# Last key tile's value products of two heads in one 256-column matmul, in free columns of the scores' PSUM tile

## The chip, the cores and the metric

The kernel runs on one core of one Trainium2 chip. The metric is the device time of one execution in microseconds (us); the time of a kernel is the median of several runs. The engines are named as in the profile: PE (TensorE, matmuls; PEld its weight loads), DVE (VectorE), ACT (ScalarE), POOL (GpSimd), and SP, whose queue starts most of the transfers. Each engine executes its instructions in the order in which the program has them, and waits at semaphores for the others.

## What is computed

One decoder layer on 512 tokens of width 2048, in float32: an RMS norm, native sparse attention (16 heads of 128 columns, 4 key and value groups), a SwiGLU feed-forward, and a final norm. The part that matters here is attention, cut down from the reference:

```python
s_c = einsum('btghd,bcgd->bghtc', q, kcc) + bias_c      # compressed keys
p_c = masked_softmax(s_c, mask_c)
o_c = einsum('bghtc,bcgd->btghd', p_c, vcc)
...
s = einsum('bqghd,bgqkd->bghqk', qc, kg) + bias         # selected keys
p = masked_softmax(s, dist >= 0)
o_s = einsum('bghqk,bgqkd->bqghd', p, vg)
...
s_w = einsum('bjqghd,bjkgd->bjghqk', qw, kwb) + bias_w  # sliding window
p_w = masked_softmax(s_w, mask_w)
o_w = einsum('bjghqk,bjkgd->bjqghd', p_w, vwb)
o = gates[0] * o_c + gates[1] * o_s + gates[2] * o_w
return o @ w_out
```

With 512 tokens both the selected and the windowed branch see every earlier key, so both are plain causal attention with a bias, each with keys and values of its own.

## The kernel before, in words

Float32 values are split into a high and a low part, and each product is made as three matmuls (`three`, lines 354 to 357): high by high, high by low, low by high. On PE's rows these are lines L355, L356 and L357 in turn; the first two use the same weights.

Heads 0 to 15 are worked through by a loop of 12 steps per head (`STEPS`), written out by hand near the end of the attention stage (lines 1039 to 1069). In one head's steps, work of three kinds is laid out:

- For the next head, `scores` (line 934) makes the score products of one query tile of 128 tokens into the PSUM tile `s`, 1536 columns wide, which exists once; DVE adds the bias and finds the maximum (L954), ACT takes the exponential (L956). Query tiles 3, 2, 1, 0 are done at steps 2, 5, 8, 11. Tile 3 fills columns 224 to 1279 of `s`, tile 2 columns 224 to 1023, tile 1 columns 736 to 1279. `finish` (line 959) scales by the gates (L967), transposes (L968) and sends the probabilities out to memory (`d_p`) on SP; `fetch` (line 972) brings them back, turned, into `ptr`.
- For the head itself, `turn` (line 981) splits the turned probabilities of one branch and one key tile into `pth` (ACT, L991) and `ptl` (DVE, L995), at steps 0 to 8; `values` (line 998) multiplies them by the values two steps later, steps 2 to 9 and 11, all into one PSUM tile `o`. The key tiles come in the order 3, 2, 1, 0, each for both branches: key tile 3 is seen by the last 128 queries alone (128 columns), key tile 2 by 256, then 384 and 512. There are three buffers of `pth` and two of `ptl`: the `ptl` of a step is written into the buffer that the value products of the same step have read. `head_out` (line 1011) copies `o` into the tile `stage` at step 11 (ACT, L1015) and SP sends it to `d_o` (heads 0 to 11).
- In between, `pump` (line 885) lays in a stretch of the dense projections (PE rows `proj`), by a count of nanoseconds per head that depends on the head and the step alone; with them go ACT's and DVE's splits of the weights (`whi`, `wlo`, L104 and L105) and, for queries and keys, a scaling into `yt` (L410) and its split.

`partial` (line 845), after the projections, makes a part of the output projection of heads 0 to 11 and stages it in a tile of 1024 columns of the same name `stage`.

Of the kernel before, what the change touches and what calls it, by code (L numbers as in the profile page):

```python
# [10 lines left out]
F32 = mybir.dt.float32  # L11
F32R = mybir.dt.float32r
I32 = mybir.dt.int32
AF = mybir.ActivationFunctionType
OP = mybir.AluOpType
# [4 lines left out]
S, D, H, DH, G, HPG = 512, 2048, 16, 128, 4, 4  # L20
NT, KC = S // 128, D // 128
# [204 lines left out]
def nsa_block(ctx: ExitStack, tc: tile.TileContext, x, rel_bias, mix_g, ffn_g, fin_g, w_in, w_out,  # L226
              pos_k, w1k, w2k, pos_v, w1v, w2v, f_in, f_out, onehot, out):
    nc = tc.nc
    mm, act, dve, pool = nc.tensor.matmul, nc.scalar.activation, nc.vector, nc.gpsimd
# [22 lines left out]
    d_o = [dram.tile([4, 128, S], F32, name=f"d_o{i}") for i in range(3)]  # L252
    d_h = dram.tile([S, 256 * N_SPILL], F32, name="d_h")
# [39 lines left out]
    def tok(t):  # L293
        return slice(128 * t, 128 * (t + 1))
# [59 lines left out]
    def three(o, ah, al, bh, bl, start, stop):  # L354
        mm(o, ah, bh, start=start, stop=False, skip_group_check=True)  # L355
        mm(o, ah, bl, start=False, stop=False, skip_group_check=True)  # L356
        mm(o, al, bh, start=False, stop=stop, skip_group_check=True)  # L357

    def ws(ps, gi, g, c0=0, c1=S, start=None, end=None, of=None):

        for u in range(2):
# [3 lines left out]
            for k in range(4):  # L365
# [5 lines left out]
                    later(lambda u=u: end(u))  # L371
                yield 650

    def later(f):
        (W.later or (lambda f: f()))(f)

# [13 lines left out]
    keep = mixer.enter_context(tc.tile_pool(name="keep", bufs=1))  # L390
# [9 lines left out]
    KK, VV, Q = {}, {}, {}  # L400
# [5 lines left out]
    kv_tiles(keep, 0)  # L406

    def normed(p, scale=1.0):
        t = keep.tile([128, S], F32, name="yt", bufs=2)
        dve.scalar_tensor_tensor(t, p, scale, ybc, op0=OP.mult, op1=OP.mult)  # L410
        return t

# [37 lines left out]
    with ExitStack() as st1:  # L450
# [4 lines left out]
        def proj_tiles(n=2):  # L455
            return [(psx if next(turns) % 4 > 1 else ps1).tile([128, 512], F32, name="proj") for _ in range(n)]
# [5 lines left out]
        with ExitStack() as st0:  # L462
# [35 lines left out]
            def bank(shape):  # L498
                return ps1.tile(shape, F32, name=next(names))
# [49 lines left out]
            p = bank([128, 512])  # L549
# [34 lines left out]
            ps = proj_tiles()  # L584
            for q in range(4):
# [23 lines left out]
                if q == 3:  # L609
                    p = bank([128, S])  # L610
# [71 lines left out]
        ps = proj_tiles()  # L682
# [3 lines left out]
        ps = proj_tiles()  # L686
# [7 lines left out]
        ps, hk = proj_tiles(), ps1.tile([128, 256], F32, name="mlp")  # L694
# [8 lines left out]
        ps = proj_tiles()  # L703
# [5 lines left out]
        ps, hv = proj_tiles(4), ps1.tile([128, 256], F32, name="mlp")  # L709
        ge = cp.tile([128, NT, 3, H], F32, name="ge")  # L710
        for i in range(8):
# [10 lines left out]
            if i == 1:  # L722
                p = ps1.tile([128, 128], F32, name="tr")
# [16 lines left out]
        ps = proj_tiles()  # L740
# [10 lines left out]
        p = ps1.tile([96, G, 128], F32, name="tr")  # L751
# [8 lines left out]
    with ExitStack() as st2:  # L760
        ap_ = st2.enter_context(tc.tile_pool(name="ap", bufs=2))
# [21 lines left out]

        W.later = lambda f: held.append((done["ns"], f))

        def stage_tile():
            return ap_.tile([128, 1024], F32, name="stage", bufs=1)

        units = iter(range(1000))

        def proj2():
            pool_ = (psx, ps2)[next(units) % 2]
            return [pool_.tile([128, 512], F32, name="proj") for _ in range(2)]
# [42 lines left out]
        def reload_o(i):  # L836

            nc.sync.dma_start(hn_l[:, i].bitcast(F32), d_o[i // 4][i % 4])

        def split_o(k):  # L840
            h, l = (x[:, 2 * k:2 * k + 2] for x in (hn_h, hn_l))
            act(h, l.bitcast(F32), AF.Copy)  # L842
            dve.tensor_tensor(l, l.bitcast(F32), h.bitcast(F32), op=OP.subtract)  # L843

        def partial(cb):
            st = stage_tile().rearrange("p (t c) -> p t c", t=NT)
            c = slice(256 * cb, 256 * (cb + 1))
            ps = [p.rearrange("p (t c) -> p t c", t=2) for p in proj2()]
            for i in range(3):
                w = W.take()  # L850
                for t in range(NT):
                    if not cb and i == 0 and t < 3:
                        reload_o(9 + t)
                    if not cb and i < 2 and t % 2 == 0:
                        later(lambda i=i, t=t: split_o(2 + 2 * i + t // 2))
                    if i == 2 and t == 2:
                        later(lambda n=W.nt + 3: W.until(n))
                    for k in range(4):
                        h = 4 * i + k
                        three(ps[t // 2][:, t % 2], hn_h[:, h, tok(t)], hn_l[:, h, tok(t)], w[0][:, k], w[1][:, k],  # L860
                              h == 0 and t % 2 == 0, h == 11)
                        if k % 2:
                            yield 650
                    if i == 2 and t % 2:
                        b = t // 2
                        act(st[:, 2 * b:2 * b + 2], ps[b], AF.Copy)
            pool.dma_start(d_h[:, c].rearrange("(t p) c -> p t c", p=128), st)
            later(pair_done)
            yield None

# [40 lines left out]

        TB, HS = {}, {}
        sc = ps2.tile([128, 3, 512], F32, name="s", bufs=1).rearrange("p a c -> p (a c)")

        def load_bias(h):
            if h < H:
# [59 lines left out]
        def arrived(rows, c0, t0, step):  # L976
            v = PT[:rows, :, c0:c0 + 32]
            p, i, c = v.ap
            return bass.AP(tensor=v.tensor, offset=v.offset, ap=[p, [step, NT - t0], i, c])

        def turn(h, b, kt):
            n = S - 128 * kt
            th = ap_.tile([128, 512], F32R, name="pth", bufs=3)
            tl = ap_.tile([128, 512], F32R, name="ptl") if b >= 0 else th
            rows = 128 if b >= 0 else 96
            if b < 0:
                src = arrived(rows, 64, 0, PT_STEP + 64)
            else:
                src = arrived(rows, PT_STEP * kt + 32 * (kt + 1) * b + 32 * kt, kt, PT_STEP + 32 * b)
            th4, tl4 = (x[:rows, :n].rearrange("p (t i s) -> p t i s", i=4, s=32) for x in (th, tl))  # L990
            act(th4, src, AF.Copy)  # L991
            if b < 0:
                dve.tensor_tensor(th4[32:64], src[32:64], th4[32:64].bitcast(F32), op=OP.subtract)
            else:
                dve.tensor_tensor(tl4, src, th4.bitcast(F32), op=OP.subtract)  # L995
            HS[h]["t", b, kt] = th[:rows, :n], tl[:rows, :n]

        def values(h, b, kt):
            s, g = HS[h], h // HPG
            first = "o" not in s  # L1000
            if first:
                s["o"] = ps2.tile([128, 512], F32, name="o", bufs=1)
            th, tl = s.pop(("t", b, kt))
            o = s["o"][:, 128 * kt:]
            if b < 0:
                mm(o, vcc[:, g], th, start=first, stop=True, skip_group_check=True)
            else:
                vh, vl = (v[:, kt, 128 * b:128 * (b + 1)] for v in VV[g % 2])
                three(o, vh, vl, th, tl, first, False)

        def head_out(h):
            o = HS[h]["o"]
            if h < 12:
                f = stage_tile()[:, :S]
                act(f, o, AF.Copy)  # L1015
                nc.sync.dma_start(d_o[h // 4][h % 4], f)
            else:
                split_from(o, hn_h[:, h], hn_l[:, h])
            del HS[h]
# [19 lines left out]
        for h in range(H):  # L1039
            seq = [(b, kt) for kt in (3, 2, 1, 0) for b in (0, 1)] + [(-1, 0)]  # L1040
            for i in range(STEPS):
                if i == 4:
                    load_bias(h + 2)
                if i == 2 and h:
                    fetch(0)
                if i < 9 and (h or i > 1):
                    turn(h, *seq[i])
                if i == 8 and h + 1 < H:
                    fetch(3)
                    fetch(2)  # L1050
                if i == 11 and h + 1 < H:
                    fetch(1)
                if i == 0 and h:
                    finish(h, 0)
                if h + 1 < H:
                    if i == 2:
                        drain_to(needed(h + 1))
                    if i % 3 == 2 and h + i > 2:
                        scores(h + 1, 3 - i // 3)
                    elif i % 3 == 0 and i:  # L1060
                        finish(h + 1, 4 - i // 3)
                if 2 <= i < 10 or i == 11:
                    if i == 2 and h % HPG == 0:
                        drain_to(h)
                    values(h, *seq[min(i - 2, 8)])
                    if i == 11:
                        head_out(h)
                if h or i > 1:
                    pump(h, i)
# [137 lines left out]

    def sub(o, a, b):
        dve.tensor_tensor(o, a, b, op=OP.subtract)  # L1209

    def plus(o, a, b):
        dve.tensor_tensor(o, a, b, op=OP.add)  # L1212

    S4 = {}

# [432 lines left out]
    n, pending = 0, None  # L1648
    for s, (b, js, _) in enumerate(PASSES):
# [6 lines left out]
        for i, j in enumerate(units):  # L1656
# [4 lines left out]
            if pending is not None:  # L1661
                o = accb["now"] = late2.tile([128, NT, 512], F32, name="accb")
# [47 lines left out]
        o = accb["now"]  # L1710
# [110 lines left out]
```

## Time and profile before

| what | value |
|---|---|
| median of 3 runs | 2091.55 us (2089.91 to 2093.0) |
| the profiled execution, its time | 2092.27 us |
| its span in the profile | 2090.5 us |
| PE busy | 2072.8 us (99%), 15220 matmuls |
| weight loads busy | 1952.6 us (93%) |
| DVE busy | 1629.2 us (78%) |
| ACT busy | 948.3 us (45%) |

The times in a timeline are counted from the start of the span. The attention loop lies between about 200 and 690 us. A matmul's row shows how long it is in flight; since matmuls overlap, what one costs in a stream is read from the distance of the starts.

### The profile page before, as it was taken

What the parts mean: (1) busy time and instruction counts of PE and PEld (TensorE: products, weight loads), DVE (VectorE), ACT (ScalarE), POOL (GpSimd) and SP (SyncE); (2) the same over time, 40 slices, a digit from 0 to 9 for tenths busy, and PEclk for the clock granted to TensorE, in tenths of its full rate; (3) what the DMA queues carried; (4) which work ended last, traced back from release to release, by engine and by line L of the source; (5) the groups of instructions that cost most, each with busy time, mean ns of one, the idle gap of its engine ahead of it and who ended that gap; (6) DMA issues with size and microseconds to landing.
All of it is one profiled execution on the core that took longest, in us unless ns stands there. A gap on an engine that the chain in (4) does not pass through costs nothing.

```text
span 2090.5 us, 39010 instructions
## 1 busy us (share of the span) xinstructions
PE 2072.8 (99%) x15220; PEld 1952.6 (93%) x15220; DVE 1629.2 (78%) x2640; ACT 948.3 (45%) x1522; POOL 275.2 (13%) x400
## 2 busy tenths in 40 slices
PE   9999999999999999999999999999999999999998
PEld 7898898898989889899999999999999999999997
DVE  5565777777786367898898888888988688697767
ACT  6344454555554234444434344334343455464445
POOL 2000011111111001022122132221211100000000
PEclk9999999999999999999999999999999999999999
DMA  7555766667677668578878688788755686685677
GB/s 239 180 148 155 195 192 195 192 198 202 201 221 212 234 204 227 164 211 230 212 214 223 190 231 218 201 229 215 199 156 151 222 265 183 198 293 156 186 208 275
DMA packets 324309, 429.77 MB, mean 206 GB/s; under 512 B 40379, under 2 KB 252027, under 8 KB 323356
## 3 DMA queue, kind: packets, MB, share of 16 engines
q1 hardware_dynamic: 263852, 295.32, 45.2%
q0 software_dynamic: 59376, 130.11, 25.8%
q8 instruction: 119, 1.95, 0.4%
q10 hardware_dynamic: 896, 1.84, 0.2%
q14 instruction: 66, 0.54, 0.1%
HBM read 364.17 MB, written 131.18 MB: 237 GB/s over the span
## 4 chain that ended last, share of the span: by engine, by line
PE 68%; DVE 1%; ACT 0%; DMA 0%; issue 0%; DVEq 0%; ACTq 0%
PE f L356 19%; PE f L355 19%; PE f L357 19%; PE proj L355 2%; PE proj L356 2%; PE proj L357 2%; PE pp L357 1%; PE pp L355 1%; PE pp L356 1%; PE po L356 1%; PE po L355 1%; PE po L357 1%; DMA tlo<-in_ffn_w_out 0%; PE pp L333 0%; DVE slot L1212 0%; PE o L356 0%
## 5 line engine op out<-in xcount | busy, mean ns | idle before, releaser
L105 DVE TENSOR_TENSOR wlo<-raw,whi 128x1024 fp32r<-128x1024 f32 (+2 forms) x223 | 247.5, 1112 | 123.0 <-ACT whi L104 122.6
L104 ACT ACTIVATE whi<-raw 128x1024 fp32r<-128x1024 f32 (+2 forms) x223 | 215.7, 971 | 224.8 <-PE f L357 70.0
L357 PE MATMUL f<-hn_h,wlo 128*128 128x256 f32 x984 | 271.6, 276 | 0.0
L355 PE MATMUL f<-hn_h,whi 128*128 128x256 f32 x984 | 271.6, 276 | 0.0
L356 PE MATMUL f<-hn_l,whi 128*128 128x256 f32 x984 | 271.6, 276 | 0.0
L1313 ACT ACTIVATE whi<-raw 128x1024 fp32r<-128x1024 f32 x123 | 126.1, 1058 | 301.6 <-DVE raw L1209 298.2
L1209 DVE TENSOR_TENSOR tlo<-tt,thi 128x1536 fp32r<-128x1536 f32 (+1 forms) x83 | 145.4, 1752 | 80.3 <-ACT thi L1318 78.7
L355 PE MATMUL proj<-hn_h,whi 128*128 128x512 f32 x504 | 200.0, 397 | 0.0
L357 PE MATMUL proj<-hn_h,wlo 128*128 128x512 f32 x504 | 196.9, 391 | 0.0
L356 PE MATMUL proj<-hn_l,whi 128*128 128x512 f32 x504 | 196.6, 390 | 0.0
L356 PEld LDWEIGHTS f<-hn_l,whi 128*128 128x128 f32 x984 | 184.7, 188 | 0.0
L355 PEld LDWEIGHTS f<-hn_h,whi 128*128 128x128 f32 x984 | 184.7, 188 | 0.0
L357 PEld LDWEIGHTS f<-hn_h,wlo 128*128 128x128 f32 x984 | 184.7, 188 | 0.0
L1318 ACT ACTIVATE thi<-tt 128x1536 fp32r<-128x1536 f32 x82 | 121.9, 1486 | 74.3 <-PE f L356 74.3
L356 PE MATMUL f<-tlo,slot 128*128 128x256 f32 (+1 forms) x546 | 151.7, 278 | 0.0
L355 PE MATMUL f<-thi,slot 128*128 128x256 f32 (+1 forms) x546 | 151.6, 278 | 0.0
L357 PE MATMUL f<-thi,slot 128*128 128x256 f32 (+1 forms) x546 | 151.6, 278 | 0.0
L357 PE MATMUL proj<-whi,hn_l 128*128 128x256 f32 (+2 forms) x496 | 146.4, 295 | 2.6 <-DVE hn_l L843 2.6
L355 PE MATMUL proj<-whi,hn_h 128*128 128x256 f32 (+2 forms) x496 | 146.6, 296 | 0.8 <-ACT hn_h L842 0.8
L1209 DVE TENSOR_TENSOR wlo<-raw,whi 128x1024 fp32r<-128x1024 f32 x123 | 147.1, 1223 | 0.0
L356 PE MATMUL proj<-wlo,hn_h 128*128 128x256 f32 (+2 forms) x496 | 145.8, 294 | 0.0
L356 PE MATMUL f<-wlo,slot 128*128 128x256 f32 (+1 forms) x432 | 121.5, 281 | 0.0
(411 smaller groups left out, 6454.5 us busy)
## 6 DMA issues: line engine op xcount, KB each, us to landing
raw<-in_ffn_w_in SPq DMA_DIRECT2D x135, 512.0 KB, 5.4
d_w<-in_ffn_w_out POOLq DMA_DIRECT2D x80, 512.0 KB, 8.8
rawx<-in_ffn_w_in SPq DMA_DIRECT2D x41, 512.0 KB, 5.3
raw<-in_ffn_w_out SPq DMA_DIRECT2D x73, 256.0 KB, 3.7
tlo<-d_w SPq DMA_DIRECT2D x73, 256.0 KB, 4.5
d_a<-d_a POOLq DMA_DIRECT2D x120, 128.0 KB, 5.8
slot<-d_a SPq DMA_DIRECT2D x18, 768.0 KB, 7.1
raw<-in_nsa_w_in POOLq DMA_DIRECT2D x24, 512.0 KB, 4.8
```

The lines of the kernel that those rows point to most:

```text
L104: self.nc.scalar.activation(hi[:, :n], src, AF.Copy)
L105: self.nc.vector.tensor_tensor(lo[:, :n], src, hi[:, :n].bitcast(F32), op=OP.subtract)
L355: mm(o, ah, bh, start=start, stop=False, skip_group_check=True)
L356: mm(o, ah, bl, start=False, stop=False, skip_group_check=True)
L357: mm(o, al, bh, start=False, stop=stop, skip_group_check=True)
L1209: dve.tensor_tensor(o, a, b, op=OP.subtract)
L1313: act(h, r, AF.Copy)
L1318: act(h, ttf, AF.Copy)
```

## The change

For heads 0 to 11 the value products of key tile 3 leave `values`. The high and low parts of an even head and the odd head behind it are put side by side into two new tiles of 512 columns (`x3` and, from the place that `stage` gives up, `stage2`). At step 4 of the odd head `last_values` makes the products of both heads, 256 columns wide, into the columns 1280 to 1535 of `s`, as six matmuls. `join_last` adds one head's 128 columns to its copy in `stage` on DVE and then sends the copy out: for the even head right behind `last_values`, for the odd head at its step 11, in `head_out`. `stage` becomes two tiles of 512 columns, and `partial` uses both, each with a transfer of its own on POOL. `yt` has one buffer instead of two.

```diff
     def normed(p, scale=1.0):
-        t = keep.tile([128, S], F32, name="yt", bufs=2)
+        t = keep.tile([128, S], F32, name="yt", bufs=1)
...
-        def stage_tile():
-            return ap_.tile([128, 1024], F32, name="stage", bufs=1)
+        def stage_tile(name="stage", dtype=F32):
+            return ap_.tile([128, 512], dtype, name=name, bufs=1)
...
         def partial(cb):
-            st = stage_tile().rearrange("p (t c) -> p t c", t=NT)
+            st = [stage_tile(x).rearrange("p (t c) -> p t c", t=2) for x in ("stage", "stage2")]
...
-                        act(st[:, 2 * b:2 * b + 2], ps[b], AF.Copy)
-            pool.dma_start(d_h[:, c].rearrange("(t p) c -> p t c", p=128), st)
+                        act(st[b], ps[b], AF.Copy)
+            for b in range(2):
+                pool.dma_start(d_h[256 * b:256 * (b + 1), c].rearrange("(t p) c -> p t c", p=128), st[b])
...
+        ox = sc[:, 1280:]
+        last = [x.rearrange("p (b n c) -> p b n c", b=2, n=2)
+                for x in (ap_.tile([128, 512], F32R, name="x3", bufs=1), stage_tile("stage2", F32R))]
...
+        def paired(h, kt):
+
+            return h < 12 and kt == 3
+
         def turn(h, b, kt):
             n = S - 128 * kt
-            th = ap_.tile([128, 512], F32R, name="pth", bufs=3)
-            tl = ap_.tile([128, 512], F32R, name="ptl") if b >= 0 else th
+            if paired(h, kt):
+                th, tl = (x[:, b, h % 2] for x in last)
+            else:
+                th = ap_.tile([128, 512], F32R, name="pth", bufs=3)
+                tl = ap_.tile([128, 512], F32R, name="ptl") if b >= 0 else th
...
+        def join_last(h):
+
+            f = outs.pop(h)
+            plus(f[:, 384:], f[:, 384:], ox[:, 128 * (h % 2):128 * (h % 2 + 1)])
+            nc.sync.dma_start(d_o[h // 4][h % 4], f)
+
+        def last_values(h):
+
+            for b in range(2):
+                three(ox, *(v[:, 3, 128 * b:128 * (b + 1)] for v in VV[h // HPG % 2]),
+                      *(x[:, b].rearrange("p n c -> p (n c)") for x in last), b == 0, b == 1)
+            join_last(h - 1)
+
         def head_out(h):
             o = HS[h]["o"]
             if h < 12:
-                f = stage_tile()[:, :S]
+                f = outs[h] = stage_tile()
                 act(f, o, AF.Copy)
-                nc.sync.dma_start(d_o[h // 4][h % 4], f)
+                if h % 2:
+                    join_last(h)
...
-                    values(h, *seq[min(i - 2, 8)])
+                    if i == 4 and h % 2 and h < 12:
+                        last_values(h)
+                    if i > 3 or h >= 12:
+                        values(h, *seq[min(i - 2, 8)])
```

The change has its own line numbers: `turn`'s split on DVE is L1009 there (L995 before), the transpose L975 (L968), the bias and maximum L961 (L954), and the sum `plus` is L375. In brackets stand the engines whose counters an instruction waits for.

DVE, head 1, from step 3 to step 5, before. The transposed tile `p_1874` is that of `finish` at step 3, the two 128x384 rows are `turn` at steps 4 and 5, and the last row begins the reductions of query tile 2's scores:

```order
L968 STREAM_TRANSPOSE p_1874<-p_1874 128x1152 [waits DVE_49]
L105 TENSOR_TENSOR wlo<-raw,whi 128x1024 [waits DMASW2_49,Activation_49]
L995 TENSOR_TENSOR ptl<-ptr,pth 128x384 [waits DMAHW1_49,PE_49,Activation_49]
L995 TENSOR_TENSOR ptl<-ptr,pth 128x384 [waits PE_49,Activation_49]
L954 ISA cx_1877,mx<-s,biasc 128x31
```

And in the change:

```order
L975 STREAM_TRANSPOSE p_1874<-p_1874 128x1152 [waits DVE_49]
L105 TENSOR_TENSOR wlo<-raw,whi 128x1024 [waits DMASW2_49,Activation_49]
L1009 TENSOR_TENSOR ptl<-ptr,pth 128x384 [waits DMAHW1_49,PE_49,Activation_49]
L375 TENSOR_TENSOR stage<-stage,s 128x128
L1009 TENSOR_TENSOR ptl<-ptr,pth 128x384 [waits PE_49,Activation_49]
L961 ISA cx_1877,mx<-s,biasc 128x31
```

The sum of head 0's last columns has come between the two `ptl`. The second `ptl` waits, as before, for PE's value products of step 5.

PE, head 1, step 4, before (the value products of key tile 2, first branch, then the dense work):

```order
L355 MATMUL o<-pth,v0h 128x256 [waits Activation_49]
L356 MATMUL o<-ptl,v0h 128x256 [waits DVE_49]
L357 MATMUL o<-pth,v0l 128x256
L355 MATMUL proj<-hn_h,whi 128x512
L356 MATMUL proj<-hn_l,whi 128x512
```

And in the change, where `x_1893` is the tile `x3` and `stage_1894` the tile `stage2`:

```order
L355 MATMUL s<-x_1893,v0h 128x256 [waits DVE_49,Activation_49]
L356 MATMUL s<-stage_1894,v0h 128x256
L357 MATMUL s<-x_1893,v0l 128x256
L355 MATMUL s<-x_1893,v0h 128x256 [waits Activation_49]
L356 MATMUL s<-stage_1894,v0h 128x256
L357 MATMUL s<-x_1893,v0l 128x256
L355 MATMUL o<-pth,v0h 128x256 [waits PE_49,Activation_49]
L356 MATMUL o<-ptl,v0h 128x256
L357 MATMUL o<-pth,v0l 128x256
L355 MATMUL proj<-hn_h,whi 128x512
```

Six matmuls into `s` have come ahead of step 4's value products; the first waits for the last reduction of query tile 3's scores. The triples `o<-pth,v0h 128x128` of steps 2 and 3 are gone.

PE, head 1, step 5, in the change (before, the rows read alike):

```order
L357 MATMUL proj<-hn_h,wlo 128x512
L355 MATMUL s<-k0h,qh 128x288 [waits DVE_49]
L356 MATMUL s<-k0l,qh 128x288
L357 MATMUL s<-k0h,ql 128x288
L355 MATMUL s<-k0h,qh 128x512
```

The score products of query tile 2 wait for DVE in both programs. Before, the count that they wait for is reached with the last reduction of query tile 3's scores; in the change it is reached with the sum at L375. The same holds in heads 3, 5, 7, 9 and 11. At step 2 of the heads behind an odd head, the score products of query tile 3 wait in the same way for the odd head's own sum.

## Rows read from the trace of the kernel before

**Rows 1.** The page, part 1: busy us (share of the span) x instructions.
```profile
PE 2072.8 (99%) x15220; PEld 1952.6 (93%) x15220; DVE 1629.2 (78%) x2640; ACT 948.3 (45%) x1522; POOL 275.2 (13%) x400
```
**Rows 2.** Window 230 to 575: us, then PE, PEld, DVE, ACT, POOL, PEclk, DMA, GB/s.
```profile
230.00:575.00 345.00, 343.34 (x1957) 302.22 (x1956) 269.88 (x709) 178.73 (x479) 49.26 (x66) 1.00 0.69 195
```
**Rows 3.** Timeline of PE, head 1, steps 3 and 4: start, us, engine, line, instruction.
```profile
251.78 0.22 PE L355 MATMUL o<-pth,v0h 128*128 128x128 f32 x1
251.84 0.27 PE L356 MATMUL o<-ptl,v0h 128*128 128x128 f32 x1
...
252.35 0.40 PE L356 MATMUL proj<-hn_l,whi 128*128 128x512 f32 x1
252.59 0.39 PE L357 MATMUL proj<-hn_h,wlo 128*128 128x512 f32 x1
...
253.50 0.28 PE L355 MATMUL o<-pth,v0h 128*128 128x256 f32 x1
...
254.09 0.39 PE L356 MATMUL proj<-hn_l,whi 128*128 128x512 f32 x1
```
**Rows 4.** Timeline, head 1: DVE's `ptl` of steps 3 to 5, PE's products of step 5.
```profile
253.66 0.43 DVE L995 TENSOR_TENSOR ptl<-ptr,pth 128x256 fp32r<-128x256 f32 x1 [1.29 <-ACT pth L991]
...
255.94 0.29 PE L355 MATMUL s<-k0h,qh 128*128 128x288 f32 x1
...
257.90 1.02 DVE L995 TENSOR_TENSOR ptl<-ptr,pth 128x384 fp32r<-128x384 f32 x2
```
**Rows 5.** Groups by shape, DVE, 205 to 575: busy us, mean ns, idle before.
```profile
L995 DVE TENSOR_TENSOR ptl<-ptr,pth 128x384 fp32r<-128x384 f32 x24 | 12.3, 549 | 0.5 <-PE o L356 0.5
...
L995 DVE TENSOR_TENSOR ptl<-ptr,pth 128x128 fp32r<-128x128 f32 x25 | 7.1, 287 | 20.2 <-ACT pth L991 20.2
```
**Rows 6.** Timeline, head 11, the two places of rows 4.
```profile
552.66 0.29 PE L355 MATMUL s<-k1h,qh 128*128 128x288 f32 x1
...
555.41 1.02 DVE L995 TENSOR_TENSOR ptl<-ptr,pth 128x384 fp32r<-128x384 f32 x2
```
**Rows 7.** Timeline of DVE, step 0 of heads 9 and 10.
```profile
485.38 0.29 DVE L995 TENSOR_TENSOR ptl<-ptr,pth 128x128 fp32r<-128x128 f32 x1 [1.51 <-ACT pth L991]
...
515.20 0.29 DVE L995 TENSOR_TENSOR ptl<-ptr,pth 128x128 fp32r<-128x128 f32 x1 [1.51 <-ACT pth L991]
```
**Rows 8.** Timeline, head 0, step 5: score products, and DVE's `ptl` of that step.
```profile
226.96 0.29 PE L355 MATMUL s<-k0h,qh 128*128 128x288 f32 x1
...
228.53 0.56 DVE L995 TENSOR_TENSOR ptl<-ptr,pth 128x384 fp32r<-128x384 f32 x1 [0.49 <-PE o L356]
```
**Rows 9.** Timeline of DVE, step 6 of heads 1 and 3.
```profile
261.40 0.69 DVE L995 TENSOR_TENSOR ptl<-ptr,pth 128x512 fp32r<-128x512 f32 x1 [1.42 <-ACT pth L991]
...
323.56 0.69 DVE L995 TENSOR_TENSOR ptl<-ptr,pth 128x512 fp32r<-128x512 f32 x1 [3.84 <-ACT pth L991]
```
**Rows 10.** Timeline of PE, behind head 12: two waits, and a slow stretch.
```profile
596.07 0.39 PE L355 MATMUL proj<-whi,hn_h 128*128 128x256 f32 x1 [0.78 <-ACT hn_h L842]
...
597.33 0.39 PE L357 MATMUL proj<-whi,hn_l 128*128 128x256 f32 x1 [0.75 <-DVE hn_l L843]
...
597.67 0.37 PE L356 MATMUL proj<-wlo,hn_h 128*128 128x256 f32 x1
...
601.04 0.32 PE L357 MATMUL proj<-whi,hn_l 128*128 128x256 f32 x1
```
**Rows 11.** Windows in that stretch, and behind a later wait (columns as in rows 2).
```profile
599.00:601.00 2.00, 2.00 (x11) 2.00 (x11) 1.61 (x8) 1.62 (x7) 0.57 (x1) 0.50 0.34 76
...
625.00:627.00 2.00, 2.00 (x19) 2.00 (x19) 0.72 (x4) 1.94 (x8) 0.00 (x0) 1.00 0.97 250
```
**Rows 12.** Waits of PE, 585 to 640: us in total, times, longest.
```profile
PE proj L357 <- DVE hn_l L843: 2.6, 4, 1.0
PE o L356 <- DVE ptl L995: 1.1, 1, 1.1
PE proj L355 <- ACT hn_h L842: 0.8, 1, 0.8
```

More of the change, by code (lines that the diff above doesn't have):

```diff
@@ L372, in ws, with plus @@
                 yield 650
+    def plus(o, a, b):
+        dve.tensor_tensor(o, a, b, op=OP.add)
     def later(f):
@@ L995, in turn @@
                 dve.tensor_tensor(tl4, src, th4.bitcast(F32), op=OP.subtract)
-            HS[h]["t", b, kt] = th[:rows, :n], tl[:rows, :n]
+            if not paired(h, kt):
+                HS[h]["t", b, kt] = th[:rows, :n], tl[:rows, :n]
         def values(h, b, kt):
@@ L1009, in values @@
                 three(o, vh, vl, th, tl, first, False)
+        outs = {}
+        def join_last(h):
[7 more added lines that the diff above has]
+            join_last(h - 1)
         def head_out(h):
@@ L1209, in sub @@
         dve.tensor_tensor(o, a, b, op=OP.subtract)
-    def plus(o, a, b):
-        dve.tensor_tensor(o, a, b, op=OP.add)
     S4 = {}
```

## The prediction, made before the change had run

> **What bounds the kernel now.** The page comes first: PE (TensorE) is busy for 99% of the span [rows 1]. The window over heads 0 to 11 says the same of the stretch that the change touches, at the full granted clock, and adds that DVE (VectorE) is busy for 270 of 345 us there [rows 2]. So PE's own work sets the time, and what the change takes from PE is gained only if nothing new makes PE wait. The third view is therefore the order of instructions with their waits (the section on the change), the fourth the timeline of PE and DVE side by side: the reader is to look, at the places where the new order has a wait, how far DVE is behind PE today.
>
> **What PE saves.** A triple of 128-column products (two of them per head) starts at 251.78 and the second projection product behind it at 252.35: 0.57 us. The same distance for a 256-column triple, 253.50 to 254.09, is 0.59 [rows 3]. Less one plain projection step (0.24, 252.35 to 252.59), a triple costs 0.33 or 0.35. A pair of heads loses four of the one and gains two of the other: 4 x 0.33 - 2 x 0.35 = 0.62 us, six pairs: **-3.7 us**, all of it PE's.
> The Trainium skill ("TensorE: Matmul & The Clock Gate", Back-to-back issue gap) gives N/2.4 + 2.5 ns per warm matmul, so its time would go with the columns and joining two would gain nothing. By that, 36 matmuls fewer would be worth about 0.1 us (an estimate from the page). The rows disagree: only a triple's first product keeps that pace (251.78 to 251.84 [rows 3]); the others take 0.11 whatever their columns.
>
> **The new wait, and its price.** `last_values` writes into the tile `s`, and `join_last` reads it on DVE, 128x128. In the built program the next score products (keys of the second-last query tile, step 5 of an odd head) wait for that sum; before, they waited for the score reductions of step 2. On DVE the sum stands behind step 4's 128x384 `ptl`, and so behind step 3's three scalings, a transpose and a weight split. In head 1 that `ptl` starts at 257.90, while PE starts the products at 255.94 [rows 4]. The sum can start 0.47 later (two `ptl` take 1.02 [rows 4], one 0.549 [rows 5]). Its own duration has no row: at least the 0 of an operation that fits into a gap, at most the 0.55 of a 128x384; I take the row of the same shape, 0.29 [rows 5]. So the products can start 257.90 + 0.76 = 258.66: **2.7 us later than now**. The six odd heads read in the same way (heads 1 and 11 are shown [rows 4, 6]) give 2.7, 3.5, 3.7, 3.6, 2.7 and 3.5, together 19.8.
>
> **How much of it adds up** depends on whether DVE is pushed back too. It isn't waiting for PE today: heads repeat after 29.8 us with the same idle stretch, ended by ACT [rows 7]. If it kept its hours, PE would be late only once, by the last value. But behind the sum stands step 5's `ptl`, whose buffer is free only when PE has done step 5's value products, and those come after the score products. Head 0 shows this chain binding already: products at 226.96, DVE let go at 228.53, so 1.57 us [rows 8]. A late PE thus delays DVE by 0.29 + 1.57 = 1.86 us in every odd head; the reductions and exponentials behind it follow. Before head 11 that is 5 x 1.86 = 9.3; with head 11's own 3.5 PE is 12.8 late. Head 3 gives some back: there DVE idles 3.84 for a late transfer where head 1 idles 1.42 [rows 9], which takes up 2.4. That makes 10.4. In even heads PE, now late, reaches `ptl`'s buffers later and pushes DVE by perhaps 1 us in two of them (heads 4 and 8, where DVE stands least behind). I take **+12 us**. PE's 3.7 us are inside: they only let it arrive earlier and wait longer. The ends are 10.4 and the plain sum 19.8 - 3.7 = 16.1.
>
> **The clock.** The new waits are about 3 us long. PE ended two waits of 0.78 and 0.75 us at 596.07 and 597.33, and then ran from 597.67 to 601.04 with products 0.41 long instead of 0.28 [rows 10], at a granted clock of 0.50, the lower level of 1.2 GHz [rows 11]: 3.4 us at half speed, 1.7 lost. After a single wait of 1.1 [rows 12] it stayed at 2.4 GHz (from 625 on [rows 11]). So I expect a fall at most of the six. Each costs the sum between 0 and 1.7; I take 1.2, since a part falls into time in which PE leads DVE: 6 x 1.2 = **+7.2 us**.
>
> **Smaller terms.** After head 11 PE waits for DVE or ACT in six places, 4.5 us in all [rows 12], because it runs ahead; with PE later by more than DVE these shrink: **-1.5 us** (between 0 and 3). The second `join_last`, at step 11, waits for ACT's copy, but DVE idles there for ACT's `pth` anyway (1.51 [rows 7]); if that cover went, six times 0.29. One buffer instead of two for `yt` costs nothing: on DVE each `yt` is followed by its own low part before the next is made. The output transfer of an even head moves on SP from behind step 11 to behind the sum of the next head's step 4; what stands behind it there, the writes of step 6, needs later DVE work anyway. On POOL each `partial` issues two transfers instead of one, each after its own ACT copy; the split of `stage` makes neither wait longer.
>
> **Sum:** 12 + 7.2 - 1.5 = +17.7 us. The profiled execution took 2092.27 (span 2090.5), 0.03% above the median of 2091.55, and the change is added to the median: **2109 us**.
>
> **Rivals.**
> (a) The waits come, the clock stays up: 10.4 to 16.1, less 1.5: +9 to +14.6, about 2103. For it: the single wait of 1.1 us [rows 12]. Against: each new wait is longer than the two that lowered the clock together.
> (b) DVE keeps its hours: PE is late by about the last value alone, 3.5, less what is given back later: 0 to +4, about 2093. For it: DVE's period is its own. Against: the buffer of step 5, which in head 0 held DVE up.
> (c) Faster: the sum is done before PE gets there. The paired heads' first two low parts no longer use `ptl`'s buffers, so DVE might run ahead; it decides if DVE comes 2.7 us earlier than now. Then the 3.7 stand alone: 2087.9. Against: the gap ahead of step 3's `ptl` (1.29) ended with ACT, not PE [rows 4], and what follows is DVE's own work back to back. Here a rule bears too: the Trainium skill ("PSUM — Partial Sum Buffer", PSUM bank collisions raise a hardware error) says to guard PSUM by bank and quadrant. By it columns 1280 to 1535 and the products of step 5 (columns 224 to 1023) need no guard between them, and the result would be this rival's; the built program holds the wait all the same.
>
> **How the numbers follow.** The forecast (waits with a falling clock) has 0.60, (a) 0.25, (b) 0.09, (c) 0.06. The range holds the first two: from 10.4 - 1.5 with 1.4 for waits that vanish later, +7.5, to 16.1 + 6 x 1.7 = +26.3: 2099 to 2118. About 0.2%, 4.2 us, can be told from no change: (b) lies within it, (c) reaches 3.7 at its best and is shared between same and faster. So faster 0.04, same 0.10, slower 0.86.
>
> **What would show it.** Right: PE rows `s` at step 5 of heads 1, 3, 5, 7, 9 and 11 with an idle stretch of some 3 us ended by DVE's `stage`; the step-5 `ptl` waiting for PE `o`; stretches at half clock behind them; triples of 128 columns gone from heads 0 to 11. Wrong: no such idle stretch (then (c)); one large stretch and small ones after (then (b)); waits with the clock at 1.0 throughout (then (a)); or PE waiting somewhere else, as at step 2 for the sum of step 11.

## The result, and the profile after

The changed kernel took **2111.98 us** (median of 5 runs, 2107.84 to 2115.02), the kernel before 2090.66 (5 runs, 2089.91 to 2093.0). The ratio is 1.0097, with a 95% interval of 1.0087 to 1.0108: 1% slower, some 21 us. The forecast was 2109 (2099 to 2118), slower. The profiled execution is the shortest of the five, 2107.84 us with a span of 2106.0, so 15.5 longer than before's 2090.5; what is known of the longer ones is told with the last experiment.

The page of the changed kernel, part 1 (busy us, share of the span, instructions), answers to [rows 1], and the window over heads 0 to 11 to [rows 2]:
```profile
PE 2071.6 (98%) x15184; PEld 1951.4 (93%) x15184; DVE 1632.3 (78%) x2652; ACT 947.8 (45%) x1522; POOL 277.9 (13%) x404
```
```profile
230.00:575.00 345.00, 327.37 (x1833) 287.50 (x1832) 261.12 (x686) 170.24 (x455) 47.75 (x64) 0.99 0.67 186
```
PE executes 36 instructions fewer, 6 for each pair of heads, and its busy time falls by 1.2 us. In the window, though, it was busy for 343.34 us before and is for 327.37 now: 16 us of the stretch have become idle. Where they went, the waits of PE over the whole span say (us in total, times, longest):
```profile
PE s L355 <- DVE stage L375: 17.6, 6, 3.3
PE proj L357 <- DVE hn_l L846: 3.3, 3, 2.4
...
PE o L356 <- DVE ptl L1009: 0.8, 1, 0.8
```
The first row is new: six waits, all of PE's score products for the sum of `join_last` (the helper's line, 375). The other two answer to [rows 12]; `hn_l` waits 3.3 in three places instead of 2.6 in four.

Head 1 and head 11 on the timeline, the places of [rows 4, 6] (start, duration, engine, line, instruction; in brackets the idle time before it and what ended it). For head 1:
```profile
257.27 0.55 DVE L1009 TENSOR_TENSOR ptl<-ptr,pth 128x384 fp32r<-128x384 f32 x1
...
257.73 0.28 DVE L375 TENSOR_TENSOR stage<-stage,s 128x128 f32<-128x128 f32 x1
...
258.07 0.40 PE L355 MATMUL s<-k0h,qh 128*128 128x288 f32 x1 [2.58 <-DVE stage L375]
...
259.77 0.56 DVE L1009 TENSOR_TENSOR ptl<-ptr,pth 128x384 fp32r<-128x384 f32 x1 [1.76 <-PE o L356]
```
and for head 11:
```profile
568.73 0.28 DVE L375 TENSOR_TENSOR stage<-stage,s 128x128 f32<-128x128 f32 x1
...
569.06 0.40 PE L355 MATMUL s<-k1h,qh 128*128 128x288 f32 x1 [2.99 <-DVE stage L375]
...
570.76 0.56 DVE L1009 TENSOR_TENSOR ptl<-ptr,pth 128x384 fp32r<-128x384 f32 x1 [1.75 <-PE o L356]
```
The reader is to see a ring. DVE's sum lets PE go; PE's value products of the step let DVE's second `ptl` go, 1.76 us late; so DVE is late in the next odd head too. The score products of step 5 started 2.1 us later than before in head 1 (258.07 against 255.94 [rows 4]) and 16.4 later in head 11 (569.06 against 552.66 [rows 6]): each pair of heads adds to it. Of the 16.4, some 4.5 are half clock, told next, and 11.9 the ring.

The clock, in windows of the profiled execution (columns as above): behind the waits of head 7 and head 9, and, for comparison, behind that of head 11.
```profile
442.50:444.50 2.00, 1.98 (x6) 1.79 (x7) 0.00 (x0) 0.00 (x0) 0.45 (x1) 0.50 1.02 231
444.50:446.50 2.00, 2.00 (x10) 1.90 (x10) 1.08 (x6) 0.38 (x2) 0.00 (x0) 0.50 0.85 239
506.50:508.50 2.00, 2.00 (x7) 1.71 (x7) 0.00 (x0) 0.00 (x0) 0.12 (x1) 0.50 1.11 214
570.00:572.00 2.00, 2.00 (x18) 1.93 (x17) 1.24 (x6) 0.47 (x3) 0.00 (x0) 1.00 1.02 191
```
0.50 is the lower level, 1.2 GHz. In this execution PE fell to it behind two of the six waits.

### The profile page after: what moved, and what is told of

Same layout as the page of the kernel before. It is cut to its first block, busy times and chain, and to the rows that moved or that the text cites. A ratio compares the mean times of both kernels' runs of the same rounds, so it can differ in the third digit from the quotient of the medians.

```text
span 2106.0 us, 38936 instructions
## 1 busy us (share of the span) xinstructions
PE 2071.6 (98%) x15184; PEld 1951.4 (93%) x15184; DVE 1632.3 (78%) x2652; ACT 947.8 (45%) x1522; POOL 277.9 (13%) x404
## 4 chain that ended last, share of the span: by engine, by line
PE 66%; DVE 1%; DMA 1%; ACT 1%; issue 0%; SPq 0%; DVEq 0%; ACTq 0%
PE f L356 18%; PE f L355 18%; PE f L357 18%; PE proj L355 2%; PE proj L356 2%; PE proj L357 2%; PE pp L355 1%; PE pp L357 1%; PE pp L356 1%; PE po L356 1%; PE po L357 1%; PE po L355 1%; DMA tlo<-d_w 1%; DMA tlo<-in_ffn_w_out 0%; PE pp L333 0%
```

## The experiments

**Is the wait alone enough?** Two kernels take the change apart from its two ends. The first is the kernel before, with one DVE sum added whose result nobody uses, and `yt` with one buffer to make room for it:

```diff
-        t = keep.tile([128, S], F32, name="yt", bufs=2)
+        t = keep.tile([128, S], F32, name="yt", bufs=1)
...
+        junk_sum = ap_.tile([128, 128], F32, name="junk_sum", bufs=1)
...
+                    if i == 4 and h % 2 and h < 12:
+                        dve.tensor_tensor(junk_sum, ybc[:, :128], sc[:, 1024:1152], op=OP.add)
                     values(h, *seq[min(i - 2, 8)])
```

> The kernel before with one buffer for yt and one added instruction in each of heads 1, 3, 5, 7, 9 and 11: at the place of the change's sum DVE adds 128 columns of s to a constant, into a tile that nothing reads. Nothing is joined, the products stay 128 wide. Theory: PE's score products of step 5 wait for it, 2 to 3 us each (0.6 less than in the change, as PE isn't ahead by its saving), and it is as slow as the change within 4 us: 2104 to 2113. Rival (the instruction costs only its own time on DVE): six times 0.2 or nothing, 2090 to 2092.

Measured: 2114.37 us (4 runs), 1.4 above the range expected, where the kernel before took 2092.14 on the same chip; ratio 1.0107 (1.0093 to 1.0121). Its waits of PE:
```profile
PE s L355 <- DVE junk_sum L1068: 15.3, 6, 2.7
```
One DVE instruction of 0.28 us, six times, costs 22 us, as much as the whole change; half-clock stretches behind four of its waits are in it. The lone sum reads columns 1024 to 1151 of `s`, and step 5's score products write columns 224 to 1023: PE waits although the two share no column; what they share is the tile. The second kernel leaves those parts of the change alone that are neither products nor sums (one `yt` buffer, `stage` split in two, two output transfers in `partial`):

```diff
-            return ap_.tile([128, 1024], F32, name="stage", bufs=1)
+            return ap_.tile([128, 512], F32, name=name, bufs=1)
...
-            pool.dma_start(d_h[:, c].rearrange("(t p) c -> p t c", p=128), st)
+            for b in range(2):
+                pool.dma_start(d_h[256 * b:256 * (b + 1), c].rearrange("(t p) c -> p t c", p=128), st[b])
```

> The kernel before with the side parts of the change alone: one buffer for yt, stage as two tiles of 512 columns, two transfers per partial. Theory: no difference, within 1 us of the kernel before. Rival (the side parts carry part of the loss, by DVE waiting for the one yt or POOL for the second transfer): 3 us or more slower.

Measured: 2092.11 (11 runs), ratio 1.0003 (0.9992 to 1.0013). They cost nothing that can be told from no change.

**Without the wait, what is the joining worth?** In the changed kernel the sum of the even head is moved from in front of step 5's score products to behind them, so that these wait for nothing new:

```diff
-            join_last(h - 1)
...
                         scores(h + 1, 3 - i // 3)
+                        if i == 5 and h % 2 and h < 12:
+                            join_last(h - 1)
```

> The change, with the even head's sum moved on DVE from ahead of step 5's second low part to behind the score reductions of step 5; all else stays. Theory (PE waits at step 5 for a sum that stands too late on DVE): the wait of PE's score products for the sum is gone in all six odd heads, no half-clock stretch between 230 and 575 us, and the saving on PE alone is left: 3.7 us under the kernel before, about 2087. Rival (the joined products, the extra sums or the moved buffers themselves cost the time): it stays at 2105 to 2112.

Measured: 2092.21 us (11 runs), ratio 1.0007 (0.9998 to 1.0015). The loss is gone, so the wait was its cause from this side too. But nothing is gained: 2087 was a miss. The second kernel makes the same products apart, 128 wide:

```diff
-                three(ox, ...)
+                for n in range(2):
+                    three(ox[:, 128 * n:128 * (n + 1)], ..., *(x[:, b, n] for x in last), ...)
```

> As the run with the later sum, but the last key tile's products of the two heads are made apart again, 128 columns each, at the same place: only the width of the matmuls differs between these two. Theory: a 128-column triple costs 0.33 and a 256-column one 0.35, so this is 3.7 us slower than the run with the later sum, level with the kernel before (2090 to 2092). Rival (a matmul's time goes by its columns): level with the run with the later sum, within 0.5.

Measured: 2090.39 (11 runs), ratio 0.9987 (0.9978 to 0.9996); not slower than the joined form but 1.8 us below it, a second miss. The waits of PE between 226 and 600 us say in part why. In the joined form:
```profile
PE s L355 <- DVE stage L375: 0.9, 2, 0.6
PE s L355 <- DVE mx L961: 0.8, 2, 0.4
...
PE o L356 <- DVE ptl L1009: 0.5, 2, 0.3
```
and in the form apart there is none of these three. The shorter work let PE run into DVE, which takes back 2.2 us of the 3.7: into the reductions, into `ptl`, and into the other sum, the one at step 11, which waits there for ACT's copy:
```profile
512.66 0.29 DVE L375 TENSOR_TENSOR stage<-stage,s 128x128 f32<-128x128 f32 x1 [1.31 <-ACT stage L1044]
...
513.00 0.40 PE L355 MATMUL s<-k0h,qh 128*128 128x288 f32 x1 [0.57 <-DVE stage L375]
```
That is not enough to put the joined form behind. In the two profiled executions it is in front, with spans of 2088.6 and 2091.7 (the latter has a half-clock stretch of 3.4 us near the start that the other lacks, up to 1.7 us lost), while its eleven runs spread from 2090.43 to 2098.86 against 2089.45 to 2093.57. Why its median is the higher one is not shown.

So the next pair moves that second sum as well, behind the score products of the next head's step 2, once joined and once apart:

```diff
                 act(f, o, AF.Copy)
-                if h % 2:
-                    join_last(h)
...
-                        if i == 5 and h % 2 and h < 12:
+                        if i == 5 and h % 2 and h < 12 or i == 2 and h % 2 == 0 and 0 < h < 13:
                             join_last(h - 1)
```

> e1 (the even head's sum behind the score products of step 5) with the odd head's sum, too, moved behind score products: from step 11 to behind those of step 2 of the next head. In e1 PE still waited 0.2 to 0.6 us at step 2 of some heads, the longest time for that second sum, 2.2 us in all with the reductions. If the waits alone ate the saving of the joined products, PE now idles under 0.5 us between 227 and 580 us and the time is 4 to 6 us under the kernel before: 2086 to 2088 where that has 2092. If the joined products save only 0.1 us, it comes out where e2 was, 2090 to 2091.

> e7 with the products made apart again, 128 wide, in the same places. If the joined ones save 0.62 us for each pair of triples, 6 pairs, it is 3.1 to 3.7 us slower than e7, with the way from the score products of step 2 to those of step 5 in odd heads 8.6 us instead of 8.0. If joining saves 0.1 us, the two are equal within 1 us and that way is the same.

Measured: 2089.82 joined (11 runs; ratio 0.9993, 0.9984 to 1.0002) and 2091.39 apart (11 runs; 0.9996, 0.9988 to 1.0005), with 2091.01 for the kernel before. Neither can be told from no change, nor are they told from each other by their intervals; both expectations were missed, 2086 to 2088 for the one and a distance of 3.1 to 3.7 (or under 1) between the two. At the place itself the difference is plain. PE in head 1, joined, from the score products of step 2 to those of step 5:
```profile
247.81 0.29 PE L355 MATMUL s<-k0h,qh 128*128 128x288 f32 x1
...
252.66 0.28 PE L355 MATMUL s<-x,v0h 128*128 128x256 f32 x1
252.78 0.28 PE L356 MATMUL s<-stage,v0h 128*128 128x256 f32 x1
...
253.37 0.28 PE L355 MATMUL o<-pth,v0h 128*128 128x256 f32 x1
...
255.80 0.29 PE L355 MATMUL s<-k0h,qh 128*128 128x288 f32 x1
```
and apart:
```profile
247.07 0.29 PE L355 MATMUL s<-k0h,qh 128*128 128x288 f32 x1
...
251.91 0.22 PE L355 MATMUL s<-x,v0h 128*128 128x128 f32 x1
251.97 0.27 PE L356 MATMUL s<-stage,v0h 128*128 128x128 f32 x1
252.08 0.28 PE L357 MATMUL s<-x,v0l 128*128 128x128 f32 x1
...
253.20 0.33 PE L355 MATMUL o<-pth,v0h 128*128 128x256 f32 x1
...
255.68 0.29 PE L355 MATMUL s<-k0h,qh 128*128 128x288 f32 x1
```
Six products of 256 columns take 0.71 us (252.66 to 253.37), twelve of 128 take 1.29 (251.91 to 253.20); the way from the score products of step 2 to those of step 5 is 7.99 us in the one and 8.61 in the other. That is the 0.62 of the prediction, and PE has about as much in each odd head (0.71 to 0.78 against 1.28 to 1.39). But the joined kernel then stands still where the other doesn't, from 226 to 600 us:
```profile
PE o L356 <- DVE ptl L1009: 1.1, 2, 0.8
...
PE s L355 <- DVE mx L961: 0.6, 1, 0.6
```
So the saving is real at its place, and at the end at most 1 to 2 us of it are left (1.6 between these two medians, 1.7 between the two profiled spans): PE, 3 us earlier, catches up with DVE's low parts and reductions.

**Is the ring closed by `ptl`'s buffer alone?** The kernel with the lone sum gets a third buffer for `ptl`, so that step 5's `ptl` needn't wait for PE's value products of that step:

```diff
-            tl = ap_.tile([128, 512], F32R, name="ptl") if b >= 0 else th
+            tl = ap_.tile([128, 512], F32R, name="ptl", bufs=3) if b >= 0 else th
```

> The kernel before with the added DVE sum of step 4 alone (as in e4, its result unused), and a third buffer for ptl, so that step 5's ptl no longer waits for PE's value products of step 5. If the push-back of DVE through ptl's buffer is what keeps the sum late head after head, the loss comes once and DVE then stays ahead: the waits after head 1's shrink to under 1 us each, in all 3 to 6 us of PE wait, 2095 to 2099 us. If the waits come from DVE's own pace and no buffer matters, it stays where e4 was, 2112 to 2116 us, with six waits of 2.3 to 2.7 us.

Measured: 2103.57 us (5 runs; before 2091.01; ratio 1.0062, 1.0049 to 1.0075), between the two theories. It loses some 10 us less than the lone sum did, 3.4 of them clock (PE fell to 1.2 GHz behind two waits instead of four, 3.4 us each time), so the buffer is part of the ring. (A third buffer without the sum was not run; before, though, DVE stood only 0.5 us at a `ptl` of this shape for PE [rows 5].) But the waits don't shrink after head 1:
```profile
PE s L355 <- DVE junk_sum L1068: 11.8, 6, 2.1
```
Head 1 on the timeline shows what holds DVE now:
```profile
258.14 0.55 DVE L997 TENSOR_TENSOR ptl<-ptr,pth 128x384 fp32r<-128x384 f32 x1
...
258.28 0.40 PE L355 MATMUL s<-k0h,qh 128*128 128x288 f32 x1 [1.99 <-DVE junk_sum L1068]
...
259.68 0.19 DVE L956 CUSTOM_DVE_ANT_0 cx<-s,biasc 128x31 f32<-128x31 f32 x1 [0.99 <-PE s L357]
```
The `ptl` follows the sum at once, and the reduction behind it waits for PE's score products, which it reads. The ring has a second path through the data itself: sum, score products, reductions of the same scores. No buffer of `ptl` opens that one.

**Is PE's work or DVE's sum the pace?** In the changed kernel the joined products of each odd head are made four times over, the last time giving the result, right ahead of the wait:

```diff
-            for b in range(2):
+            for i in range(8):
+                b = i % 2
                 three(ox, ...)
```

> The changed kernel with the six joined products of each odd head made four times over (the last time gives the result; 18 more matmuls, by 0.114 us apart 2.06 us of PE work per odd head, 12.3 in all, straight ahead of the wait). If the wait for DVE's sum sets the pace there, the added work lies inside it: the idle before the score products of step 5 falls from 2.6 to 3.3 us to some 0.5 to 1.2, the end moves by 0 to 3 us only (2108 to 2114), and the clock does not fall behind these waits. If PE's own work sets the pace, it costs its full 12 us: 2122 to 2125.

Measured: **2105.09 us** (5 runs, 2103.94 to 2106.94; before 2091.01; ratio 1.0064, 1.005 to 1.0078). With more work for PE it is not slower than the changed kernel but faster, below the range expected too: the intervals of the two ratios don't meet. In head 1 the 24 products take 2.87 us, where the six took 0.71; over the six odd heads 13.0 us are added (12.3 were planned).
```profile
252.51 0.28 PE L355 MATMUL s<-x,v0h 128*128 128x256 f32 x1
...
255.38 0.28 PE L355 MATMUL o<-pth,v0h 128*128 128x256 f32 x1
```
The waits of PE, one of the six, and the window over heads 0 to 11:
```profile
PE s L355 <- DVE stage L375: 5.1, 6, 1.3
```
```profile
258.05 0.28 DVE L375 TENSOR_TENSOR stage<-stage,s 128x128 f32<-128x128 f32 x1
...
258.39 0.40 PE L355 MATMUL s<-k0h,qh 128*128 128x288 f32 x1 [0.42 <-DVE stage L375]
```
```profile
226.00:600.00 374.00, 368.87 (x2114) 325.13 (x2113) 286.34 (x753) 186.70 (x501) 50.74 (x68) 1.00 0.68 190
```
The wait fell from 17.6 to 5.1 us, by 12.5, for 13.0 us of added work: DVE's hour sets the pace, and most of PE's work ahead of it is free. Not all: the span of this profile, 2105.1, is 2 to 4 us above those of the unfilled kernel less what half clock cost them (table below). The clock stayed at 1.00 behind all six waits, and the mean granted clock of the five runs is 0.998 to 0.999, where the unfilled kernel's five have 0.994 to 0.995. The 4.5 to 9.4 us that half clock costs the unfilled kernel in its profiles are enough for the 6.9 between the medians.

**How often does the clock fall?** The changed kernel was profiled twice more, with nothing altered.

> The changed kernel once more, nothing altered, for a second profile. If the clock's falls behind the six waits are a matter of chance, other heads than 7 and 9 show them, between one and five of the six, and the time goes with them: about 2104 plus 1.3 to 2.4 us for each. If heads 7 and 9 are special (they come right behind a weight stage's change), the falls are in the same two.

> The changed kernel a third time, as e9: two profiles more, to see whether the heads in which the clock falls differ from execution to execution, with the waits themselves (2.5 to 3.3 us each) the same.

Measured: 2114.51 us (span 2112.7) and 2113.65 (span 2111.8), with the same waits (17.1 us in six, both). The windows behind the waits of head 7 and head 9, in the second profile:
```profile
447.00:449.00 2.00, 2.00 (x14) 1.88 (x14) 0.31 (x1) 0.00 (x0) 0.44 (x1) 1.00 0.98 255
...
508.00:510.00 2.00, 1.94 (x6) 1.75 (x7) 0.01 (x1) 0.00 (x0) 0.49 (x1) 0.50 1.05 232
510.00:512.00 2.00, 2.00 (x8) 1.71 (x7) 1.04 (x4) 0.34 (x2) 0.00 (x0) 0.50 0.85 223
512.00:514.00 2.00, 2.00 (x6) 1.52 (x6) 0.58 (x4) 1.94 (x7) 0.00 (x0) 0.50 0.73 277
```
and behind that of head 1 in the third:
```profile
259.00:261.00 2.00, 2.00 (x7) 1.71 (x8) 0.00 (x0) 0.00 (x0) 0.07 (x1) 0.50 1.09 219
261.00:263.00 2.00, 2.00 (x8) 1.71 (x7) 1.37 (x6) 0.60 (x3) 0.00 (x0) 0.50 0.83 250
```
The 6.8 us stretches begin while PE still stands, as in head 3 of the second profile, where PE starts at 320.57 only:
```profile
320.00:320.50 0.50, 0.00 (x0) 0.00 (x0) 0.50 (x2) 0.00 (x0) 0.24 (x1) 0.50 0.74 136
```
Half clock costs nothing there, so what is lost is half of the part in which PE works. Read in windows of 0.5 us, the stretches at 0.50 behind the six waits are:

| profile | heads, length in us | time lost (half of it, without the waits) | span over before's | rest |
|---|---|---|---|---|
| first | 7 (6.8), 9 (3.4) | 4.5 | 15.5 | 11.0 |
| second | 3 (6.8), 5 (3.4), 9 (6.8), 11 (3.4) | 9.4 | 22.2 | 12.8 |
| third | 1 (6.8), 3 (3.4), 7 (6.8), 9 (3.4) | 9.3 | 21.3 | 12.0 |

Which waits lower the clock differs from execution to execution, with waits of the same length. Heads 7 and 9 are not a pair of their own; head 9 is in all three, each of the others in one or two, and three profiles can't tell whether that is more than chance. The rest is nearly the same in all three. So the loss has two parts: 11 to 13 us of DVE's and PE's ring, and 4 to 9 us of half clock.

The other four of the five runs lie 2.5 to 7.2 us above the first profile and have no trace, but their mean granted clock is on record: 0.995 for three, as for the profiled one, and 0.994 for the longest. A thousandth of the span is 2.1 us, so more half clock can explain at most some 2 us of the distance of the three, and 2 to 4 of the longest one's 7.2. What the remainder is stays open.

## Why the prediction was right

The measured change is 21.3 us between the medians, against 17.7 foreseen.

**The place and the wait.** Right in all six heads, and nowhere else. In head 1 the sum started 0.46 us behind its `ptl` (0.47 foreseen) and took 0.28 (0.29), and PE came 2.1 us late (2.7): the `ptl` itself started 0.63 earlier than before (257.27 against 257.90 [rows 4]).

**The push-back.** Right, and a little small. In heads 1, 3, 5 and 11 DVE's `ptl` starts 1.70 us behind the first score product (258.07 to 259.77 in head 1), where the reading of head 0 gave 1.57 [rows 8]; DVE idles 1.75 to 1.77 there, and 2.96 in the half-clock stretches of heads 7 and 9. Head 3's late transfer took up what was foreseen: the 3.84 of [rows 9] is now
```profile
324.59 0.69 DVE L1009 TENSOR_TENSOR ptl<-ptr,pth 128x512 fp32r<-128x512 f32 x1 [1.42 <-ACT pth L1005]
```
that is, 2.4 less. Heads 4 and 8 pushed DVE as foreseen, but by another way than `ptl`'s buffers: the score reductions of step 2 waited for PE's products, as here in head 8.
```profile
468.63 0.19 DVE L961 CUSTOM_DVE_ANT_0 cx<-s,biasc 128x31 f32<-128x31 f32 x1 [1.78 <-PE s L357]
```
PE's lateness in head 11, without half clock, is the 11.9 us named above, against +12. With the -1.5 of the later waits the forecast makes +10.5; the rest in the table is 11.0 to 12.8. The -1.5 was too large: the later waits went from 4.5 us [rows 12] to 4.1 (the 3.3 and 0.8 above). What the prediction did not see is that the ring has a second path: it named the buffer as the chain, and with a third buffer most of the waiting stayed (11.8 of 15.3 us).

**The clock.** A term right in sum and wrong in its parts. Foreseen were falls behind most of the six waits, up to 1.7 us each, together 7.2. Measured were two, four and four, at 1.7 or 2.8 to 3.1 each, together 4.5, 9.4 and 9.3. The step that failed is the reading of the one stretch of [rows 10] as the length of every stretch: it can last 6.8 us too. That 7.2 lies between the sums is in part luck: fewer falls than foreseen, and half of them dearer.

**What PE saves.** Inside the wait, as foreseen, and worth nothing there. Measured by itself, 0.62 us for the first pair of heads (7.99 against 8.61), the term read from [rows 3] holds. Rival (c)'s price, though, took the 3.7 us to stand alone at the end once the wait was gone, and that failed: the waits that come next (for the other sum, the reductions, `ptl`) take most of it.
By the formula that the prediction took from the Trainium skill ("TensorE: Matmul & The Clock Gate", Back-to-back issue gap), the two widths would cost nearly the same for each column. The traces don't agree: starts are 0.11 us apart at 128 columns and 0.12 at 256, and only the first product of a run of 128 keeps 0.06. The prediction left out that the same section of the Trainium skill calls this the gap of an isolated matmul and gives 81 ns at 128 columns and 131 at 512 for a stream with weight loads; that points the right way, but the traces have 0.11 and 0.23 us.

**The side parts.** `yt`, `stage` and the transfers cost nothing, as foreseen. The sum at step 11 took the place of the `pth` wait of [rows 7], with 1.31 us of idle instead of 1.51:
```profile
278.54 0.29 DVE L375 TENSOR_TENSOR stage<-stage,s 128x128 f32<-128x128 f32 x1 [1.31 <-ACT stage L1045]
```

**The rivals.** (a), waits without the clock, was shown by the kernel with filled waits, and lies where it was put: 2105 against about 2103, though with 13.0 us more work, most of which lies in the waits. (b), DVE keeping its hours, fell: even with a third buffer it doesn't. Whether the sum and the products of step 5 need a guard between them, which (c) touches, was not tried: in every kernel here the two share one tile, and none gives the sums a tile of their own. It stays open.

## What to carry to other kernels

Before work is put into spare space of a tile, list who else reads and writes that tile, on which engine, and how far each is behind: a 0.28 us instruction on the follower, placed between two steps of the leader, cost some 20 us because each then waited for the other in every round. An operation whose result is wanted late belongs behind the leader's next use of the tile, not in front of it. And a leader that is made faster gains only the follower's distance; here 3.7 us of saved matmuls were worth 1 to 2 at best. Idle time that can't be taken out can be worth filling: here the clock then stayed up.

## What the runs showed of the hardware that was not expected

The same wait of 2.5 to 3.3 us lowered TensorE's clock in some executions and not in others: 10 of 18 times in the three profiles of the changed kernel. A stretch at 1.2 GHz lasted 3.4 or 6.8 us, nothing between: the five of 6.8 began while PE still stood, 0.6 to 1.2 us before the wait's end, the five of 3.4 within 0.2 us of it. Where PE did redundant products until it had only 0.4 to 1.3 us left to wait, the granted clock stayed at 1.00 behind all six waits, and a kernel with 13.0 us more matmul work ended 7 us sooner (2105.09 against 2111.98).
